# Scores of a gated linear recurrence in tiles of 32 keys on TensorE

## The chip, the cores and the metric

The kernel runs on one core of a Trainium2 chip. The metric is the device time of one execution in microseconds, the median of several runs. A core has a matmul engine (TensorE, PE in the profile, with its weight loads as PEld), VectorE (DVE), ScalarE (ACT), GpSimd (POOL), SyncE (SP, which issues most transfers here) and 16 DMA engines. Matmuls read from SBUF and write to PSUM, both with 128 partitions.

## What is computed

One block of a hybrid network on 1040 tokens (16 meta tokens and 1024 tokens) of width 1024: a layer norm, one large input projection, two recurrences side by side (HGRN2 with 8 heads of 128 keys and 128 values, mLSTM with 4 heads), their gated output projections, a layer norm, a mixture of 64 experts with 8 per token, and a last layer norm. The change touches only the first recurrence. For one head and one chunk of tokens it is, with `b` the running sum of the logarithms of the forget gate:

```python
b = jnp.cumsum(lfc, axis=2)
o_inter = jnp.einsum('bhtk,bhkv->bhtv', qc * jnp.exp(b), state)
rel = b[:, :, :, None, :] - b[:, :, None, :, :]
decay = jnp.exp(jnp.where(causal[:, :, None], rel, -jnp.inf))
scores = jnp.einsum('bhtk,bhsk,bhtsk->bhts', qc, kc, decay)
o = o_inter + jnp.einsum('bhts,bhsv->bhtv', scores, vc)
```

The decay depends on key, query and channel at once, so the scores are no plain matrix product of `q` and `k`.

## The kernel before

The kernel works on chunks of 128 tokens, 8 to a head, all 8 in one instruction where it can. Tokens lie on the free axis, the 128 key channels on the partitions. It splits the causal pairs of a chunk into levels. At level `lv` (block size B = 2^lv) the chunk is cut into blocks of B tokens; a query in an odd block meets the keys of the even block just ahead of it. Query and key are scaled by products of gates up to the border of the two blocks (`pre` and `suf`, which grow from level to level), so that the scores of a level are a plain matrix product. Level 0 (a query and the key one before it) and the diagonal (a query and its own key) are done together ahead of the loop.

*Diagonal and level 0* (line 699 to 706). `qx` holds for each chunk 128 queries and behind them the 64 odd queries times their gate, 192 columns. Line 704 multiplies all 128 keys of a chunk with all 192 columns, two chunks to a PSUM tile of the pool "sc" (`ps_sc()`, two buffers in turn), four groups a head. Lines 705 and 706 copy out of PSUM under a mask (`copy_predicated`) into `st`, the matrix of scores of the head: the diagonal from the first 128 columns, level 0 from the other 64.

*Levels 1 to 6* (line 707 on). Line 724 forms the scaled queries `qp` of the odd blocks, 64 a chunk, and line 726 the scaled keys of the even blocks in a tile `ks` whose other columns are zero or stale. Line 738 multiplies them: at levels 1 to 4 all 128 keys with all 64 queries of a chunk, 8 matmuls a level; at level 5 two matmuls a chunk, with 32 keys and 32 queries each, onto partitions 0 to 31 and 64 to 95 of PSUM; at level 6 one matmul a chunk with 64 keys and 64 queries, onto partitions 0 to 63. Levels 1 to 4 go through a masked copy of the whole tile on VectorE (line 741), since most of the 128 x 64 products of a chunk belong to no pair of that level: with blocks of up to 16 tokens, keys 32w to 32w+31 only meet the odd-block queries 16w to 16w+15. Levels 5 and 6 are copied by ScalarE (746, 747 and 749). Lines 752 to 756 carry `pre` and `suf` on to the next level, on VectorE. All these operands are float32.

Behind the levels, lines 767 to 798 turn the keys, carry the state from chunk to chunk and form the output of the head (line 790 reads `st`).

The order of the work is set by a planner when the kernel is built: it simulates the engines and takes, on each engine, the ready instruction of the highest priority. Each engine then runs its instructions in that order. PE's projections (lines 135 to 145, `mm3` and `mm_packed`, in `natural_slab`, `f_slab`, `q_slab`) are ready most of the time, and stand between the bursts of score matmuls. Heads 0 to 3 run beside the projections of the second half of the columns, heads 4 to 7 beside those of the second recurrence.

Of the kernel before, what the change touches and what calls it, by code (L numbers as in the profile page):

```python
# [14 lines left out]
AF = mybir.ActivationFunctionType  # L15
# [4 lines left out]
P = 128  # L20
# [51 lines left out]
def block_kernel(tc, A, out):  # L72
    nc = tc.nc
# [176 lines left out]
    def stage_tile():  # L250
        return stage.tile([P, 512], F32, name="st", tag="st", bufs=6)
# [325 lines left out]
    def ps_sc():  # L577
        return psum.tile([P, 512], F32, name="sc", tag="sc", bufs=2)
# [94 lines left out]
        nc.vector.tensor_mul(og, hn[:, :, 0:256], og)  # L673
        nc.sync.dma_start(tok(yB[:, hs]), og)

    def hgrn_head(h, kss, st, zero):
        hp = slice(h * P, (h + 1) * P)
        f = rt([P, L], "a0")
        qx = rt([P, 8, 192], "a1")
        q = qx[:, :, 0:P]  # L680
        nc.sync.dma_start(f, fT[hp, :])
        nc.sync.dma_start(q, qT[hp, :].rearrange("p (c t) -> p c t", t=P))
        v = rt([P, 8, P], "v")
        vm = rt([NM, P], "vm")
        g = rt([P, 8, P], "g")
        nc.sync.dma_start(v, tok(vA[NM:L, hp]))
        nc.sync.dma_start(vm, vA[0:NM, hp])
        nc.sync.dma_start(g, tok(gA[:, hp]))
        k = rt([P, L], "a2")
        nc.vector.tensor_scalar(k, f, -1.0, 1.0, op0=OP.mult, op1=OP.add)  # L690
        km = rt([P, NM], "km")
        nc.vector.memset(km[:, NM - 1:NM], 1.0)
        nc.vector.tensor_tensor_scan(km[:, NM - 2::-1], f[:, NM - 1:0:-1], zero[:, :NM - 1], 1.0, op0=OP.mult, op1=OP.add)
        nc.vector.tensor_mul(km, km, k[:, 0:NM])
        pre = f[:, NM:L].rearrange("p (c t) -> p c t", t=P)
        kx = k[:, NM:L].rearrange("p (c t) -> p c t", t=P)
        suf = rt([P, 8, P], "a3")

        nc.vector.tensor_mul(qx[:, :, P:], q[:, :, 1::2], pre[:, :, 1::2])
        for gg in range(4):  # L700
            sc = ps_sc()[:, 0:384].rearrange("p (c t) -> p c t", t=192)
            cs = slice(2 * gg, 2 * gg + 2)
            for i in range(2):
                nc.tensor.matmul(sc[:, i], kx[:, 2 * gg + i], qx[:, 2 * gg + i], start=True, stop=True)
            nc.vector.copy_predicated(st[:, cs], lmask[:, 5, 0:256].rearrange("p (c t) -> p c t", t=P), sc[:, :, 0:P])
            nc.vector.copy_predicated(st[:, cs, 1::2], lmask[:, 0, 0:128].rearrange("p (c t) -> p c t", t=64), sc[:, :, P:])
        for lv in range(7):
            B = 1 << lv
            N = 512 // B

            def sp(t):
                r = t.rearrange("p c (n w b) -> p (c n) w b", w=2, b=B)
                return r[:, :, 0, :], r[:, :, 1, :]

            p0, p1 = sp(pre)
            s0, s1 = sp(suf)
            if lv == 0:
                nc.gpsimd.tensor_copy(s0, p1)
                nc.gpsimd.memset(s1, 1.0)
                nc.vector.tensor_mul(p1, p1, p0[:, :, B - 1:B].to_broadcast([P, N, B]))  # L720
                continue
            qp = rt([P, N, B], "qp", 2)
            odd = [r.rearrange("p c (n w b) -> p c n w b", w=2, b=B)[:, :, :, 1] for r in (q, pre)]
            (nc.gpsimd if lv in QP_POOL else nc.vector).tensor_mul(qp.rearrange("p (c n) b -> p c n b", c=8), *odd)
            ks = kss[lv % 2]
            nc.vector.tensor_mul(sp(ks)[0], sp(kx)[0], s0)
            sc = ps_sc()
            qpf = qp.rearrange("p n b -> p (n b)")
            for c in range(8):
                t64 = c * 64  # L730
                if lv == 6:
                    spans = ((0, 64, 0, 64),)
                elif lv == 5:
                    spans = ((0, 32, 0, 32), (64, 96, 32, 64))
                else:
                    spans = ((0, P, 0, 64),)
                for a, b, u, v_ in spans:
                    nc.tensor.matmul(sc[a:b, t64 + u:t64 + v_], ks[:, c, a:b], qpf[:, t64 + u:t64 + v_],
                                     start=True, stop=True)
            if lv < 5:  # L740
                nc.vector.copy_predicated(sp(st)[1], lmask[:, lv].rearrange("p (n b) -> p n b", b=B),
                                          sc.rearrange("p (n b) -> p n b", b=B))
            else:
                scc = sc.rearrange("p (c t) -> p c t", t=64)
                if lv == 5:
                    nc.scalar.activation(st[0:32, :, 32:64], scc[0:32, :, 0:32], AF.Copy)
                    nc.scalar.activation(st[64:96, :, 96:128], scc[64:96, :, 32:64], AF.Copy)
                else:
                    nc.scalar.activation(st[0:64, :, 64:128], scc[0:64], AF.Copy)
            if lv == 6:  # L750

                nc.vector.tensor_mul(s1, s1, sp(kx)[1])
                nc.vector.tensor_mul(s0, sp(ks)[0], p1[:, :, B - 1:B].to_broadcast([P, N, B]))
            else:
                nc.vector.tensor_mul(s0, s0, p1[:, :, B - 1:B].to_broadcast([P, N, B]))
            nc.vector.tensor_mul(p1, p1, p0[:, :, B - 1:B].to_broadcast([P, N, B]))
        nc.vector.tensor_mul(q, q, pre)
        pt = ps_tr()
        nc.tensor.transpose(pt[:NM, 0], km, ident)
        knm = rt([NM, P], "knm")  # L760
        nc.scalar.activation(knm, pt[:NM, 0], AF.Copy)
        kn = rt([P, 8, P], "a5")
        for gg in range(2):
            n = 4 if gg == 0 else 3
            pt = ps_tr()
            for i in range(n):
                nc.tensor.transpose(pt[:, i], suf[:, 4 * gg + i], ident)
            nc.scalar.activation(kn[:, 4 * gg:4 * gg + n], pt[:, :n], AF.Copy)
        sts = rt([P, 8, P], "a2")
        pt = ps_tr()  # L770
        nc.tensor.matmul(pt[:, 0], knm, vm, start=True, stop=True)
        nc.vector.tensor_copy(sts[:, 0], pt[:, 0])
        for gg in range(2):
            n = 4 if gg == 0 else 3
            pt = ps_tr()
            for i in range(n):
                c = 4 * gg + i
                nc.tensor.matmul(pt[:, i], kn[:, c], v[:, c], start=True, stop=True)
            for i in range(n):
                c = 4 * gg + i  # L780
                nc.vector.scalar_tensor_tensor(sts[:, c + 1], sts[:, c], pre[:, c, P - 1:P], pt[:, i],
                                               op0=OP.mult, op1=OP.add)
        sq = rt([P, P], "sq", 2)
        ss = rt([P, 3, 8], "ss", 2)
        for gg in range(2):
            po = ps_tr() if gg else ps_o().rearrange("p (c t) -> p c t", t=P)
            s4 = slice(4 * gg, 4 * gg + 4)
            for i in range(4):
                c = 4 * gg + i
                nc.tensor.matmul(po[:, i], st[:, c], v[:, c], start=True, stop=False)  # L790
                nc.tensor.matmul(po[:, i], q[:, c], sts[:, c], start=False, stop=True)
            for i in range(4):
                nc.scalar.activation(sq, po[:, i], AF.Square, accum_out=ss[:, 0, 4 * gg + i:4 * gg + i + 1])
            nc.vector.tensor_scalar(ss[:, 1, s4], ss[:, 0, s4], 1.0 / P, EPS, op0=OP.mult, op1=OP.add)
            rsqrt(ss[:, 2, s4], ss[:, 1, s4], (P, 4))
            for i in range(4):
                c = 4 * gg + i
                nc.vector.scalar_tensor_tensor(g[:, c], po[:, i], ss[:, 2, c:c + 1], g[:, c], op0=OP.mult, op1=OP.mult)
        nc.sync.dma_start(tok(yA[:, hp]), g)
# [4 lines left out]
    with tc.tile_pool(name="reca", bufs=1) as rec:  # L804
# [2 lines left out]
        sts_ = [rec.tile([P, 8, P], F32, name=f"st{i}") for i in range(1)]  # L807
        for t in kss + sts_ + [zero]:
            nc.gpsimd.memset(t, 0.0)
        lm = stage_tile()[:, 0:384].rearrange("p (v t) -> p v t", t=64)  # L810
        nc.sync.dma_start(lm, A["lmask"])
        for lv in range(5):
# [4 lines left out]
        for s in range(2):  # L817
            if s:
                natural_slab(IA + s * 512, copy_out(vA, s * 512), True)
            natural_slab(GA + s * 512, gate_out(gA, s * 512, A["hg_norm_g"], True), False, None if s else slab_ga)  # L820
            f_slab(s)
            q_slab(s)
            for h in range(4):
                hgrn_head(4 * s + h, kss, sts_[0], zero)
        for s in range(2):
            natural_slab(VB + s * 512, copy_out(vB, s * 512), True)
            natural_slab(OB + s * 512, gate_out(oB, s * 512, A["ml_norm_g"], False), False)
# [713 lines left out]
    with man:  # L1541
# [10 lines left out]
        for t in range(N + 1):  # L1552
# [8 lines left out]
            if cur:  # L1561
                r = order[t][0]
# [296 lines left out]
```

## Time and profile before

| | |
|---|---|
| runs (3) | median 2410.21 us, 2406.28 to 2413.15 us |
| profiled execution | 2406.26 us, of which span 2404.5 us |
| PE busy | 2318.2 us, 96% of the span, 12754 matmul records |
| weight loads (PEld) | 1860.0 us, 77% |
| VectorE | 1587.8 us, 66% |
| ScalarE | 1106.7 us, 46% |
| GpSimd | 392.6 us, 16% |
| mean granted clock of PE | 0.984 |

The span is the time from the first to the last instruction. Busy time of PE counts a matmul from its start to its modelled end, and neighbours overlap, so a busy engine can still be made faster by shorter matmuls. A row of a timeline gives start, duration, engine, line, operation, tiles and shapes, and how many instructions were merged; a group's duration runs to the end of its last instruction. `128*32 128x32` is a matmul with 128 contraction rows, 32 weight columns and 32 moving columns.

### The profile page before, as it was taken

What the parts mean: (1) busy time and instruction counts of PE and PEld (TensorE: products, weight loads), DVE (VectorE), ACT (ScalarE), POOL (GpSimd) and SP (SyncE); (2) the same over time, 40 slices, a digit from 0 to 9 for tenths busy, and PEclk for the clock granted to TensorE, in tenths of its full rate; (3) what the DMA queues carried; (4) which work ended last, traced back from release to release, by engine and by line L of the source; (5) the groups of instructions that cost most, each with busy time, mean ns of one, the idle gap of its engine ahead of it and who ended that gap; (6) DMA issues with size and microseconds to landing.
All of it is one profiled execution on the core that took longest, in us unless ns stands there. A gap on an engine that the chain in (4) does not pass through costs nothing. (4 is left out here: it accounts for less than half of the span.)

```text
span 2404.5 us, 35446 instructions
## 1 busy us (share of the span) xinstructions
PE 2318.2 (96%) x12754; PEld 1860.0 (77%) x12754; DVE 1587.8 (66%) x3143; ACT 1106.7 (46%) x1848; POOL 392.6 (16%) x270
## 2 busy tenths in 40 slices
PE   6999999999999999999999999999999999999992
PEld 4788888988878987788788877777777777777761
DVE  8621888158812656412577596888888888888884
ACT  3432222221222246421332323777777777776773
POOL 3200000000000000000000001233434434444421
PEclk9989999999999999999999999999999999999996
DMA  7232333322323246526354425999999999999995
GB/s 277 89 106 88 106 111 115 119 93 89 102 96 107 79 160 206 175 97 216 129 201 144 135 85 188 299 334 317 337 324 327 312 333 321 314 324 322 306 291 157
DMA packets 203490, 476.71 MB, mean 198 GB/s; under 512 B 18721, under 2 KB 67553, under 8 KB 203313
## 3 DMA queue, kind: packets, MB, share of 16 engines
q1 hardware_dynamic: 181040, 396.24, 47.0%
q0 software_dynamic: 21520, 75.51, 13.4%
q10 hardware_dynamic: 752, 2.69, 0.3%
q8 instruction: 101, 1.65, 0.3%
q14 instruction: 77, 0.62, 0.1%
HBM read 372.16 MB, written 103.78 MB: 198 GB/s over the span
## 5 line engine op out<-in xcount | busy, mean ns | idle before, releaser
L197 DVE TENSOR_TENSOR wl<-wraw,wh 128x1024 fp32r<-128x1024 f32 x118 | 141.5, 1220 | 219.4 <-ACT wh L196 215.3
L136 PE MATMUL mm<-hL,wh 128*128 128x512 f32 (+2 forms) x768 | 278.0, 362 | 0.0
L137 PE MATMUL mm<-hH,wl 128*128 128x512 f32 (+2 forms) x768 | 277.5, 361 | 0.0
L135 PE MATMUL mm<-hH,wh 128*128 128x512 f32 (+2 forms) x768 | 277.0, 361 | 0.0
L1441 POOL DMA_INDIRECT acc<-yo,idx x95 | 193.3, 2035 | 504.3 <-DMA acc<-yo,idx 108.4
L137 PE MATMUL mm<-wh,hL 128*128 128x512 f32 x512 | 209.7, 410 | 6.3 <-DVE hL L346 6.3
L136 PE MATMUL mm<-wl,hH 128*128 128x512 f32 x512 | 209.4, 409 | 2.5 <-DVE wl L284 2.5
L135 PE MATMUL mm<-wh,hH 128*128 128x512 f32 x512 | 211.0, 412 | 0.6 <-DVE xr L534 0.6
L135 PEld LDWEIGHTS mm<-hH,wh 128*128 128x128 f32 x768 | 144.4, 188 | 17.1 <-issue 0.9
L136 PEld LDWEIGHTS mm<-hL,wh 128*128 128x128 f32 x768 | 144.4, 188 | 16.3 <-issue 0.5
L137 PEld LDWEIGHTS mm<-hH,wl 128*128 128x128 f32 x768 | 144.6, 188 | 15.6 <-issue 0.2
L196 ACT ACTIVATE wh<-wraw 128x1024 fp32r<-128x1024 f32 x118 | 122.7, 1056 | 57.9 <-PE mm L136 37.7
L1508 DVE TENSOR_TENSOR wl<-eraw,wh 128x1024 fp32r<-128x1024 f32 x112 | 134.9, 1215 | 17.0 <-ACT wh L1507 16.6
L1362 POOL DMA_INDIRECT xg<-h,idx x95 | 136.1, 1432 | 48.7 <-issue 23.5
L1508 DVE TENSOR_TENSOR wl<-wraw,wh 128x1024 fp32r<-128x1024 f32 x96 | 115.7, 1215 | 27.1 <-ACT wh L1507 26.7
L135 PE MATMUL mm<-wh,xh 128*128 128x512 f32 (+3 forms) x296 | 123.4, 417 | 0.0
L1507 ACT ACTIVATE wh<-eraw 128x1024 fp32r<-128x1024 f32 x112 | 117.0, 1060 | 13.6 <-PE mm L137 9.1
L137 PEld LDWEIGHTS mm<-wh,hL 128*128 128x128 f32 x512 | 98.6, 192 | 30.4 <-DVE hL L346 9.0
L137 PE MATMUL mm<-wh,xl 128*128 128x512 f32 (+3 forms) x296 | 116.6, 394 | 0.0
L136 PE MATMUL mm<-wl,xh 128*128 128x512 f32 (+3 forms) x296 | 116.5, 394 | 0.0
L136 PEld LDWEIGHTS mm<-wl,hH 128*128 128x128 f32 x512 | 98.8, 193 | 22.8 <-DVE wl L284 3.0
L135 PEld LDWEIGHTS mm<-wh,hH 128*128 128x128 f32 x512 | 99.0, 193 | 22.0 <-PE mm L530 0.8
(547 smaller groups left out, 5540.6 us busy)
## 6 DMA issues: line engine op xcount, KB each, us to landing
eraw<-in_wexp_dram SPq DMA_DIRECT2D x210, 512.0 KB, 7.7
wraw<-in_wexp_dram SPq DMA_DIRECT2D x168, 512.0 KB, 7.5
wraw<-in_w_in_dram SPq DMA_DIRECT2D x72, 512.0 KB, 5.0
sgT<-st SPq DMA_DIRECT2D x32, 256.0 KB, 2.5
sg<-sgT SPq DMA_DIRECT2D x32, 256.0 KB, 3.2
wraw<-in_w_branch_a_dram SPq DMA_DIRECT2D x16, 512.0 KB, 4.7
wraw<-in_w_branch_b_dram SPq DMA_DIRECT2D x16, 512.0 KB, 5.2
wraw<-in_w_out_dram SPq DMA_DIRECT2D x16, 512.0 KB, 4.0
```

The lines of the kernel that those rows point to most:

```text
L135: nc.tensor.matmul(o, ah, bh, start=start, stop=False)
L136: nc.tensor.matmul(o, ah, bl, start=False, stop=False)
L137: nc.tensor.matmul(o, al, bh, start=False, stop=stop)
L196: nc.scalar.activation(h, raw, AF.Copy)
L197: (nc.gpsimd if j in on_pool else nc.vector).tensor_sub(l, raw, h.bitcast(F32))
L1362: nc.gpsimd.indirect_dma_start(out=self.x, out_offset=None, in_=h1[:, :], in_offset=bass.IndirectOffsetOnAxis(ap=self.idx, axis=0))
L1441: self.out = nc.gpsimd.indirect_dma_start(out=acc[:, :], out_offset=bass.IndirectOffsetOnAxis(ap=self.idx, axis=0), in_=self.y, in_offset= ...
L1507: nc.scalar.activation(h, raw, AF.Copy)
L1508: (nc.gpsimd if j in POOL_SPLITS else nc.vector).tensor_sub(l, raw, h.bitcast(F32))
```

## The change

The scores of the diagonal and of levels 1 to 4 are computed in pieces of 32 keys, with only the queries that belong to those keys: four matmuls a chunk with 32 weight columns and 16 query columns at a level, eight a chunk (four with 32 query columns for the diagonal, four with 16 for level 0) ahead of the loop. Piece `w` writes partitions 32w to 32w+31 of PSUM. Level 6 keeps its matmul and puts odd chunks on partitions 64 to 127, so that ScalarE copies even and odd chunks apart. The products that no longer are computed leave parts of the PSUM tile unwritten; the tiles are therefore two fixed ones (`scs`), set to zero once, and no longer taken in turn from the pool: a group or level takes the one of its parity.

```diff
-    def hgrn_head(h, kss, st, zero):
+    def hgrn_head(h, kss, st, zero, scs):
...
         for gg in range(4):
-            sc = ps_sc()[:, 0:384].rearrange("p (c t) -> p c t", t=192)
+            sc = scs[gg % 2][:, 0:384].rearrange("p (c t) -> p c t", t=192)
             cs = slice(2 * gg, 2 * gg + 2)
             for i in range(2):
-                nc.tensor.matmul(sc[:, i], kx[:, 2 * gg + i], qx[:, 2 * gg + i], start=True, stop=True)
+                c = 2 * gg + i
+                for a, b in ((0, 32), (P, 16)):
+                    for w in range(4):
+                        r, u = slice(32 * w, 32 * w + 32), slice(a + b * w, a + b * w + b)
+                        nc.tensor.matmul(sc[r, i, u], kx[:, c, r], qx[:, c, u], start=True, stop=True)
...
-            sc = ps_sc()
+            sc = scs[lv % 2]
...
                 else:
-                    spans = ((0, P, 0, 64),)
+                    spans = tuple((32 * w, 32 * w + 32, 16 * w, 16 * w + 16) for w in range(4))
                 for a, b, u, v_ in spans:
-                    nc.tensor.matmul(sc[a:b, t64 + u:t64 + v_], ks[:, c, a:b], qpf[:, t64 + u:t64 + v_],
+
+                    o = 64 if lv == 6 and c % 2 else 0
+                    nc.tensor.matmul(sc[a + o:b + o, t64 + u:t64 + v_], ks[:, c, a:b], qpf[:, t64 + u:t64 + v_],
                                      start=True, stop=True)
...
-                    nc.scalar.activation(st[0:64, :, 64:128], scc[0:64], AF.Copy)
+                    for j in range(2):
+                        nc.scalar.activation(st[0:64, j::2, 64:128], scc[64 * j:64 * j + 64, j::2], AF.Copy)
...
+        scs = [ps_sc() for _ in range(2)]
+        for t in scs:
+            nc.vector.memset(t, 0.0)
...
-                hgrn_head(4 * s + h, kss, sts_[0], zero)
+                hgrn_head(4 * s + h, kss, sts_[0], zero, scs)
```

## Rows read from the trace of the kernel before

**Rows 1.** The page: busy time of PE; the granted clock in 40 slices.
```profile
PE 2318.2 (96%) x12754; PEld 1860.0 (77%) x12754; DVE 1587.8 (66%) x3143; ACT 1106.7 (46%) x1848; POOL 392.6 (16%) x270
...
PEclk9989999999999999999999999999999999999996
```

**Rows 2.** Table by stretches: length, busy us by engine (instructions), clock, DMA share, GB/s.
```profile
244.00:397.00 153.00, 151.84 (x1043) 127.93 (x1041) 128.46 (x305) 33.27 (x93) 4.21 (x7) 1.00 0.33 102
...
504.00:655.00 151.00, 149.65 (x1032) 125.86 (x1031) 125.98 (x301) 33.24 (x93) 3.63 (x6) 1.00 0.34 106
655.00:1400.00 745.00, 741.52 (x3553) 612.64 (x3553) 369.32 (x780) 248.15 (x429) 1.08 (x3) 1.00 0.42 143
```

**Rows 3.** Waits of VectorE, 244 to 655 us: total us, times, longest.
```profile
DVE st L741 <- PE sc L738: 25.3, 28, 1.4
```

**Rows 4.** Groups by form, PE, 244 to 655 us: busy us, mean ns, idle.
```profile
L738 PE MATMUL sc<-qp,kss 128*128 128x64 f32 x512 | 60.9, 273 | 0.6 <-DVE qp L724 0.2
...
L738 PE MATMUL sc<-qp,kss 128*64 128x64 f32 x128 | 9.2, 225 | 0.0
L738 PE MATMUL sc<-qp,kss 128*32 128x32 f32 x256 | 5.6, 197 | 0.0
```

**Rows 5.** PE's timeline around a burst of levels 1 to 4: start, duration, instruction.
```profile
294.28 0.40 PE L135 MATMUL mm<-wh,hH 128*128 128x512 f32 x1
294.51 0.39 PE L136 MATMUL mm<-wl,hH 128*128 128x512 f32 x1
...
296.76 0.39 PE L135 MATMUL mm<-wh,hH 128*128 128x512 f32 x1
```

**Rows 6.** PE's timeline around both diagonal bursts of head 1 (line 704).
```profile
280.30 0.40 PE L137 MATMUL mm<-wh,hL 128*128 128x512 f32 x1
...
282.07 0.39 PE L136 MATMUL mm<-wl,hH 128*128 128x512 f32 x1
...
282.76 0.39 PE L136 MATMUL mm<-wl,hH 128*128 128x512 f32 x1
...
284.79 0.40 PE L135 MATMUL mm<-wh,hH 128*128 128x512 f32 x1
```

**Rows 7.** PE's timeline around a burst of level 6.
```profile
350.08 0.39 PE L137 MATMUL mm<-wh,hL 128*128 128x512 f32 x1
350.41 1.15 PE L738 MATMUL sc<-qp,kss 128*64 128x64 f32 x16
...
351.82 0.38 PE L767 MATMUL tr<-ident,a 128*128 128x128 f32 x2
```

**Rows 8.** PE's timeline around a burst of level 5.
```profile
346.94 0.40 PE L136 MATMUL mm<-wl,hH 128*128 128x512 f32 x1
347.26 0.70 PE L738 MATMUL sc<-qp,kss 128*32 128x32 f32 x32
...
348.23 0.39 PE L135 MATMUL mm<-wh,hH 128*128 128x512 f32 x1
```

**Rows 9.** Stretches of 10 ns, line 738: PE, PEld; x counts instructions under way.
```profile
347.26:347.27 0.01, 0.01 (x1) 0.01 (x2) 1.00 0.53 205
...
350.46:350.47 0.01, 0.01 (x1) 0.01 (x2) 1.00 0.00 0
```

**Rows 10.** Line 749 (copies of level 6): ns minimum, median, maximum.
```profile
L749 ACT ACTIVATE st<-sc x8: 591/592/595, 267.3 to 652.8; 64x512 f32<-64x512 f32 x8
```

**Rows 11.** VectorE's timeline: masked copies of two successive levels, in brackets the idle time.
```profile
292.57 0.70 DVE L741 COPY_PREDICATED st<-lmask,sc 128x512 f32<-128x512 uint8 x1 [0.83 <-PE sc L738]
...
296.68 0.71 DVE L741 COPY_PREDICATED st<-lmask,sc 128x512 f32<-128x512 uint8 x1 [0.76 <-PE sc L738]
```

**Rows 12.** Timelines of VectorE and PE, head 2: last diagonal copies, burst of level 1.
```profile
325.13 0.72 DVE L706 COPY_PREDICATED st<-lmask,sc 128x128 f32<-128x128 uint8 x2
...
326.29 0.33 PE L738 MATMUL sc<-qp,kss 128*128 128x64 f32 x2
```

**Rows 13.** PE's timeline: a burst of matmuls of one column (line 929).
```profile
1444.26 0.34 PE L929 MATMUL po<-ones,selb 128*128 128x1 bf16 x8
```

## The prediction

> **What bounds the kernel now.** [...] The changed function runs in two stretches, heads 0 to 3 at 244 to 397 us and heads 4 to 7 at 504 to 655 us. PE is busy 151.8 of 153 us and 149.7 of 151 us in them, and 741.5 of 745 us in the stretch behind them [rows 2]. VectorE (DVE) comes second, 128 of 153 us and 126 of 151 us. The list of who waited for whom confirms it: in and between both stretches DVE waited 25.3 us for the score matmuls of levels 1 to 4 (28 times) [rows 3]. So PE is the bound, in and behind the changed part, and a microsecond of PE time taken out there should come off the end. How much PE time the scores hold is the whole question.
>
> Busy time does not answer it, since matmuls overlap (a record of a 64-column pass lasts 273 ns, 512 of them would be 140 us and are 60.9 us busy [rows 4]). I take the price of a burst of score matmuls from PE's timeline: from the start of the last projection matmul ahead of it to the start of the second one behind it, less 0.46 us for those two, which lie 0.23 us apart in a plain stream [rows 5]. It contains what the burst does to its neighbours.
>
> Every float32 matmul shows as two weight loads and two passes: the 256 matmuls of levels 1 to 4 give 512 records [rows 4].
>
> **Prices before.** A level of 1 to 4: 294.51 to 296.76 is 2.25, less 0.46: 1.79 us for 16 passes of 128 weight columns [rows 5]. There are 32 of these (8 heads, 4 levels). The diagonal: 280.30 to 282.07 gives 1.31 us, 282.76 to 284.79 gives 1.57 us, mean 1.44 us for 8 passes of 192 query columns [rows 6]; two such bursts a head, 16 in all. Level 6: 350.08 to 351.82 gives 1.28 us for 16 passes of 64 weight columns [rows 7]; 8 in all. Level 5 is not changed, and is the row to learn from: it already writes tiles of 32 keys, on partitions 0 and 64 in turn. 346.94 to 348.23 gives 0.83 us for 32 passes [rows 8], of which (0.70 - 0.197) = 0.50 us is the passes themselves (from the first one's start to the last one's; one lasts 197 ns [rows 4]) and 0.33 us the change from and to the full-width matmuls. That is 15.8 ns a pass, where a level of 1 to 4 takes 1.79/16 = 112 ns.
>
> **Do tiles of 32 keys run side by side?** The onset of the two bursts tells it. At level 5 two weight loads are under way in the first 10 ns; at level 6, all on one tile, the second one joins 50 to 60 ns behind the burst's start at 350.41 [rows 7, 9]. By the order of the code the first two loads of level 5 would be the two passes of the same 32 keys. Had they shared one tile, the second would have come as late as at level 6 does, scaled to 32 columns. So I read the pair as the first passes of the tiles at partitions 0 and 64: each tile goes through its own passes at 0.50/16 = 31.5 ns, and the two tiles go at once.
>
> **The change, part by part.** *Levels 1 to 4.* 8 matmuls become 32, four tiles by 8 chunks: 64 passes, 16 to a tile, exactly what each tile of level 5 gets, with 16 query columns instead of 32. If four tiles go at once as two do, a level costs what level 5 costs: 0.83 us. Saved: 0.96 x 32 = 30.7 us. *Diagonal.* Two groups are 4 chunks of 8 matmuls, 64 passes, again 16 to a tile: 0.83 us; saved (1.44 - 0.83) x 16 = 9.8 us. *Level 6.* As many matmuls, now on partitions 0 and 64 in turn: half of 15 steps (1.15 - 0.225 = 0.93 us [rows 4, 7]) is 0.46 us; x 8 = 3.7 us. Sum 44.2 us of PE time.
>
> *Edits at next to nothing.* ScalarE copies level 6 in two pieces instead of one of 592 ns [rows 10]; that adds less than another 592 ns a head, on an engine that is busy 33 of 153 us [rows 2]. Two memsets of a score tile on DVE come once, ahead of the first head, and only its first scores wait for them; by the copies of 512 columns (0.70 us [rows 11]) they are 1.4 us if uncovered. The masked copies from PSUM keep their shapes. PE's stream grows by 152 matmuls a head, 2432 passes and as many loads in all. No DMA is added or moved.
>
> *One buffer order changes.* The diagonal's last group and level 1 now share a score tile, so level 1 waits for that group's four masked copies. In head 2 these end at 325.13 + 0.72 = 325.85 and level 1's burst begins at 326.29 [rows 12]: covered by 0.44 us now, and the diagonal ends sooner after the change. Queued behind that wait would be projection matmuls. I take 0; uncovered, four copies (1.5 us) x 8 heads is 12 us.
>
> **Bounds of the unknown price.** No row has four tiles at once. Above: passes issue no closer than level 5's average of 15.8 ns. Below: half the query columns shorten the passes, and a tile's 31.5 ns could shrink up to half, 0.25 us a level or 8 to 10 us in all. I take the tile's own pace, since the onset [rows 9] shows passes 10 ns apart or less and nothing there that two tiles share.
>
> **Rivals.**
> *Issue pace.* If 15.8 ns is what PE can issue, 64 passes take 1.01 + 0.33 = 1.34 us. Saved: 0.45 x 32 + 0.10 x 16 + 3.7 = 19.7 us. For it: level 5's 64 instructions may have been queued while PE was busy, and 128 in a row are nowhere in the trace.
> *A new wait.* From one level's masked copy to the next DVE works 3.4 of 4.11 us (292.57 to 296.68; five operations of 0.68 to 0.70 us, the first and the next copy stand in the rows) and waits 0.76 us for PE [rows 11]. PE spends 1.79 us of the 4.11 on the burst; with 0.83 us and the same projection matmuls it would be round in 3.15 us, and wait 0.3 us for DVE: 9.6 us of 32 levels, leaving 34.6 us. Against it: the planner sets the order anew and has projection matmuls to put in.
> *The floor (slower).* A pass never starts less than 25 ns behind the last one. For it: eight 1-column matmuls of the router take (0.34 - 0.163)/7 = 25 ns each [rows 13]. Then 64 passes take 1.60 + 0.33 = 1.93 us: 0.14 x 32 + 0.49 x 16 - 3.7 = 8.6 us lost. It decides from 22 ns on, where 48 x (64 passes + 0.33 us) equals the 84 us of today, level 6's gain included. Against it: level 5's 15.8 ns. The router's matmuls all use one tile. [...]
> *The tiles do not run side by side* (the change does not do what it says): 64 x 31.5 ns + 0.33 = 2.35 us, 0.56 x 32 + 0.91 x 16 = 32.5 us lost, level 6 gaining nothing. Level 5 speaks against it.
> *Nothing arrives.* The new order of the planner delays a projection or its weights by as much as is saved. Against it: no idle stretch of PE lies behind the part [rows 2].
>
> **How the numbers follow.** The profiled execution took 2406.26 us, the median of the runs is 2410.21, 3.95 us more. Forecast: 2406.26 - 44.2 = 2362.1, on the median 2366 us; chance 0.45. New wait: 2376, 0.18. Issue pace: 2390, 0.18. Nothing arrives: 2410, 0.08. The floor: 2419, 0.07. No side by side: 2443, 0.04. The range goes from 2356 (the shorter pass) to 2398 (issue pace with some waiting), and leaves out the last three, 0.19. About 0.3%, 7 us, is what a measurement of this kernel can tell from no change: faster 0.81, same 0.08, slower 0.11.
>
> **What would show it.** The burst of levels 1 to 4 should last some 0.7 us with 64 passes, the diagonal's as long, level 6 about 0.7 us; PE should count 2432 more matmuls and wait as little as now; the second stretch should end about 44 us earlier, and what follows keep its length. Bursts of 1.2 us mean the issue pace, of 1.8 us the floor. PE waiting for DVE at the score lines means the new wait. The prediction is wrong if the bursts shrink and the end does not move.

## The result, and the profile after

The changed kernel took 2380.8 us (median of 4 runs, 2374.28 to 2384.78), the kernel before beside it 2411.68 us: ratio 0.9873, 95% interval 0.985 to 0.9896, or 30.6 us less (this and all such figures below go by the ratio). The direction was right and the time lies in the range; of the 44 us forecast, 14 are missing. The profiled execution took 2378.61 us, its span 2376.8 us, 27.7 us less than before.

The page of the changed kernel, PE's line and the granted clock in 40 slices:

```profile
PE 2277.3 (96%) x15186; PEld 1808.1 (76%) x15186; DVE 1587.0 (67%) x3145; ACT 1106.6 (47%) x1856; POOL 385.9 (16%) x270
...
PEclk9989999999999999999999999999999999999996
...
q8 instruction: 120, 1.97, 0.3%
```

PE counts 2432 more matmul records than in [rows 1], as expected, and is 40.9 us less busy. That is more than the 27.7 us by which the span fell, so PE must now wait somewhere. The table by stretches (columns as in [rows 2]) shows where:

```profile
244.00:397.00 153.00, 145.91 (x2261) 114.11 (x2258) 131.08 (x312) 36.99 (x101) 4.17 (x7) 0.98 0.35 108
504.00:655.00 151.00, 146.46 (x2046) 115.75 (x2045) 129.01 (x330) 40.31 (x116) 3.61 (x6) 1.00 0.37 114
655.00:1400.00 745.00, 738.75 (x3542) 609.41 (x3541) 380.25 (x847) 246.04 (x420) 1.08 (x3) 1.00 0.42 141
```

In [rows 2] PE was idle 1.2 and 1.4 us in these two stretches; now it is idle 7.1 and 4.5 us. The third row no longer holds the same work as before; counted from the start of the last score matmul to the end, PE is idle 62.3 us where it was 60.6, so most of the new idle time lies in the two stretches. The list of PE's waits in the same stretches (line waited for: us in total, times, longest), all of it:

```profile
PE sc L708 <- DMA a<-qT: 6.1, 5, 1.5
PE sc L744 <- issue: 4.6, 3, 3.8
PE sc L708 <- DVE kss L730: 0.7, 1, 0.7
PE sc L744 <- DVE qp L728: 0.5, 3, 0.2
```

Two of them are new and large: the diagonal (line 708) waits for the load of the queries, and the levels (line 744) wait for "issue", which is nothing that the profile names.

PE's timeline around one burst of levels 1 to 4, and around one of level 6 (start, duration, instruction; compare [rows 5, 7]):

```profile
295.44 0.40 PE L135 MATMUL mm<-wh,hH 128*128 128x512 f32 x1
295.77 0.74 PE L744 MATMUL sc<-qp,kss 128*32 128x16 f32 x64
...
296.78 0.40 PE L137 MATMUL mm<-wh,hL 128*128 128x512 f32 x1
...
304.96 0.40 PE L135 MATMUL mm<-wh,hH 128*128 128x512 f32 x1
305.29 0.69 PE L744 MATMUL sc<-qp,kss 128*64 128x64 f32 x16
...
306.24 0.39 PE L137 MATMUL mm<-wh,hL 128*128 128x512 f32 x1
```

Priced as in the prediction, a level costs 296.78 - 295.44 - 0.46 = 0.88 us (median of 28 bursts 0.87), where 0.83 was forecast and 1.79 was paid. Its 64 passes begin within 0.55 us, on average one every 0.55/64 = 8.6 ns. Level 6 costs 306.24 - 304.96 - 0.46 = 0.82 us (forecast 0.81, before 1.28). Both shapes do what they were meant to do.

Now the two waits. First the diagonal of head 1: SyncE's issue of the queries' load, then PE.

```profile
276.81 0.57 SPq L682 DMA_DIRECT2D a<-qT  x1
...
280.56 0.39 PE L137 MATMUL mm<-wh,hL 128*128 128x512 f32 x1
281.69 0.33 PE L708 MATMUL sc<-a,a 128*32 128x32 f32 x16 [0.74 <-DVE kss L730]
...
282.29 0.39 PE L136 MATMUL mm<-wl,hH 128*128 128x512 f32 x1
...
283.19 0.61 PE L708 MATMUL sc<-a,a 128*32 128x16 f32 x48
```

Sixteen passes that take 0.14 us cost 282.29 - 280.56 - 0.46 = 1.27 us, because the queries land 4.7 us behind their issue (at 281.56 us) and PE stands in front of them. (The bracket names a VectorE instruction; the other five of these waits are put down to the load itself. In all six heads this first burst starts 0.14 us behind the landing in the trace.) The diagonal of a head is now three bursts, of 16, 48 and 64 passes, instead of two.

Second, head 0, in PE's timeline:

```profile
247.81 1.18 PE L744 MATMUL sc<-qp,kss 128*32 128x16 f32 x79
252.78 0.93 PE L744 MATMUL sc<-qp,kss 128*32 128x16 f32 x49 [3.79 <-issue]
...
254.23 0.63 PE L137 MATMUL mm<-wh,hL 128*128 128x512 f32 x1
254.66 0.63 PE L135 MATMUL mm<-wh,hH 128*128 128x512 f32 x1
```

The stretches ahead of the stop and behind it, in the table by stretches, PE alone (length, busy us, instructions, granted clock, DMA share, GB/s):

```profile
244.00:248.90 4.90, 4.68 (x158) 1.00 0.94 289
252.70:258.10 5.40, 5.32 (x60) 0.50 0.02 5
```

Levels 1 and 2 stand back to back here, 128 passes, and PE stops 3.79 us in their middle. Behind the stop the granted clock is 0.50 for 5.4 us: projection matmuls lie 0.43 us apart instead of 0.23.

The prices of all bursts, summed for each kernel by the prediction's method (us; stops and waits inside a burst are part of its price):

| kernel | diagonal | levels 1 to 4 | level 6 | sum | span | span less sum |
|---|---|---|---|---|---|---|
| before | 22.8 | 59.3 | 10.2 | 92.3 | 2404.5 | 2312.2 |
| after | 23.4 | 34.7 | 6.6 | 64.7 | 2376.8 | 2312.1 |
| levels only (e1) | 25.6 | 28.0 | 6.5 | 60.1 | 2373.4 | 2313.3 |
| diagonal only (e2) | 24.3 | 59.3 | 10.2 | 93.8 | 2406.5 | 2312.7 |
| queries in two buffers (e3) | 16.5 | 32.8 | 6.5 | 55.8 | 2370.4 | 2314.6 |
| level 1 of two heads whole (e4) | 26.7 | 32.8 | 6.6 | 66.1 | 2378.2 | 2312.1 |
| tile after tile (e5) | 27.0 | 68.5 | 6.6 | 102.1 | 2416.0 | 2313.9 |
| tiles of 64 (e6) | 25.2 | 41.1 | 6.6 | 72.9 | 2385.6 | 2312.7 |
| e1 and two buffers (e7) | 23.0 | 28.8 | 6.5 | 58.3 | 2371.7 | 2313.4 |
| e3 and e4 (e8) | 17.1 | 32.7 | 6.5 | 56.3 | 2371.1 | 2314.8 |
| e3, two diagonals whole (e9) | 17.5 | 28.2 | 6.6 | 52.3 | 2362.2 | 2309.9 |
| e3, instructions shifted (e10) | 16.4 | 33.6 | 6.5 | 56.5 | 2374.9 | 2318.4 |
| before, two buffers (e11) | 23.9 | 57.5 | 10.2 | 91.6 | 2399.1 | 2307.5 |

The last column is nearly constant (2312 to 2315 in ten of the thirteen, 2307.5 to 2318.4 in all): to within some 5 us, a microsecond of burst price is a microsecond of span. The clock outside the changed part also differs between single executions: ahead of the first head the mean granted clock was 0.76 before and 0.80 after from 120 to 155 us, and from 0 to 244 us 0.94 before, 0.95 after, 0.98 in e7 and 0.97 in e9. That it explains the rest is not shown: e7, with the highest, has 2313.4 in the last column. So the forecast's frame holds, and the question is the terms: the diagonal saved -0.6 us instead of 9.8, the levels 24.6 instead of 30.7, level 6 3.6 of 3.7.

### The profile page after: what moved, and what is told of

Its sections match the earlier page's. It is cut to its first block, busy times and chain, and to the rows that moved or that the text cites. A ratio compares the mean times of both kernels' runs of the same rounds, so it can differ in the third digit from the quotient of the medians.

```text
span 2376.8 us, 40262 instructions
## 1 busy us (share of the span) xinstructions
PE 2277.3 (96%) x15186; PEld 1808.1 (76%) x15186; DVE 1587.0 (67%) x3145; ACT 1106.6 (47%) x1856; POOL 385.9 (16%) x270
## 5 line engine op out<-in xcount | busy, mean ns | idle before, releaser
L135 PEld LDWEIGHTS mm<-wh,hH 128*128 128x128 f32 x512 | 98.8, 193 | 22.8 <-PE mm L530 1.1
```

The source lines that it names most:

```text
L135: nc.tensor.matmul(o, ah, bh, start=start, stop=False)
```

## Experiments

**Which part gained.** The change was split in two.

e1, the diagonal undone:

```diff
-                for a, b in ((0, 32), (P, 16)):
-                    for w in range(4):
-                        r, u = slice(32 * w, 32 * w + 32), slice(a + b * w, a + b * w + b)
-                        nc.tensor.matmul(sc[r, i, u], kx[:, c, r], qx[:, c, u], start=True, stop=True)
+                nc.tensor.matmul(sc[:, i], kx[:, c], qx[:, c], start=True, stop=True)
```

> Levels 1 to 4 in tiles of 32 keys and level 6 on two tiles in turn, as in the change; the diagonal as before, one matmul of 192 query columns a chunk. Theory A (the diagonal's share of the gain was eaten by a new wait for the next head's queries): the diagonal costs what it cost before, 22.8 us of PE time, as its pieces cost now with their waits (23.4 us), so this kernel keeps the whole gain, 27 to 31 us under the kernel before. Rival B (the diagonal does give its 10 us, and as much was lost somewhere in the levels): 17 to 20 us under the kernel before.

Measured: 2375.51 us, ratio 0.986 (0.9843 to 0.9877), 33.7 us less than before. Leaving the diagonal's tiles out costs nothing (the intervals of this kernel and of the whole change overlap). Its whole diagonals cost 25.6 us, 2.8 more than before: PE waits 2.4 us, in five places, for the product of line 699, which follows the queries; before, it was 0.4 us once. The stop in head 0 is gone too; its two levels back to back, in PE's timeline:

```profile
246.92 1.59 PE L741 MATMUL sc<-qp,kss 128*32 128x16 f32 x128
```

e2, the levels undone (diagonal alone):

```diff
-                    spans = tuple((32 * w, 32 * w + 32, 16 * w, 16 * w + 16) for w in range(4))
+                    spans = ((0, P, 0, 64),)
...
-                    o = 64 if lv == 6 and c % 2 else 0
+                    o = 0
...
```

> Only the diagonal in tiles of 32 keys; levels 1 to 4 and 6 as before. Theory A (new wait for the queries): no gain, within 3 us of the kernel before, and PE waits 1 to 2 us ahead of the first diagonal burst of six heads. Rival B: 8 to 10 us under the kernel before.

Measured: 2404.76 us, ratio 0.9977 (0.9966 to 0.9989), 5.5 us less. In its trace the diagonal gains nothing (24.3 us) and its span is 2 us longer than before; the profiled execution, 2408.31 us, lies near the upper end of its runs. PE's wait list has the same new row:

```profile
PE sc L708 <- DMA a<-qT: 7.7, 5, 2.0
```

So the gain of the diagonal's tiles is eaten in the diagonal itself, by waiting for queries. The 5.5 us of the runs lie between the two expectations, and the trace doesn't show where they come from.

**The wait for the queries.** `qx` has one buffer, so a head's queries can be called for only when the last output matmul of the head ahead has read them (276.39 us for head 0, issue at 276.81). e3 gives `qx` a second buffer and finds room for it in another tile:

```diff
-        qx = rt([P, 8, 192], "a1")
+        qx = rt([P, 8, 192], "a1", 2)
...
+        qps = rt([P, 2, 512], "a5")
...
-            qp = rt([P, N, B], "qp", 2)
+            qp = qps[:, lv % 2].rearrange("p (n b) -> p n b", b=B)
```

> The changed kernel with two buffers for the query tile, so that the next head's queries can be loaded before the last matmul of this head has read its own (room is made by putting the two query products of the levels into the tile that later takes the turned keys). Theory A: the wait ahead of the first diagonal burst (some 7 to 9 us over six heads) goes, so 6 to 10 us under the changed kernel, 36 to 41 us under the kernel before. Rival (PE waits there for VectorE, which is late with the keys, and not for the load): no change against the changed kernel.

Measured: 2365.66 us, ratio 0.9823 (0.9809 to 0.9837), 42.7 us less than before (36 to 41 expected). The row of the queries has left PE's wait list; this is all of it:

```profile
PE sc L745 <- issue: 3.8, 2, 3.4
PE sc L709 <- DVE a L690: 1.3, 3, 0.8
PE sc L745 <- DVE a L729: 0.2, 1, 0.2
```

The diagonal's price falls from 23.4 to 16.5 us. Two controls ask whether the second buffer, and not the diagonal, brought this. e7 is e1 with two buffers:

> The diagonal undone (whole matmuls of 128 keys and 192 queries) and the queries in two buffers: the same as the run with the queries in two buffers but for the diagonal. Theory A (the diagonal's tiles are worth what was forecast once the queries lie ready, less the stop for instructions in head 0): slower than that run by 5 to 10 us, about 2371 to 2376 us, -34 to -39 us to the kernel before, hardly other than without the second buffer (2375.5 us), since whole diagonal matmuls waited little for the queries. Rival B (the second buffer of the queries by itself brings the gain, and the diagonal's tiles bring none): equal to that run, about 2366 us.

Measured: 2372.83 us, ratio 0.9841 (0.9824 to 0.9858). By the trace the diagonal's tiles are now worth 23.0 - 16.5 = 6.5 us, of which the stop in head 0 takes back 4.0 (levels 28.8 against 32.8); the runs differ by 7 us with overlapping intervals. The whole diagonals, 25.6 us in e1, are back at 23.0. e11 is the kernel before with two buffers:

> The kernel before with the queries in two buffers and nothing else. Theory A (the wait for the queries came only with the change, since the whole diagonal needed the product of line 699 and was placed later): 0, within 3 us of the kernel before. Rival B (the second buffer is a gain of its own, and the run with the change and two buffers owes it that): -6 to -12 us.

Measured: 2404.31 us, ratio 0.9989 (0.9975 to 1.0003): no change that can be told, and a gain of more than 6 us is excluded. The second buffer is worth something only where the change has put the wait.

**Four tiles at once.** e5 computes the same 32 matmuls of a level in another order, all chunks of one tile, then the next tile:

```diff
-            for c in range(8):
...
-                for a, b, u, v_ in spans:
+            for c, (a, b, u, v_) in ([(c, s) for s in spans for c in range(8)] if lv < 5 else [(c, s) for c in range(8) for s in spans]):
```

> The kernel of the change with one edit: at levels 1 to 4 the loop over the four tiles stands outside and the loop over the eight chunks inside, so that the same 32 matmuls come tile after tile instead of the four tiles in turn. Theory A (the 8.6 ns a pass come from four tiles at work at once, and they are that only because consecutive matmuls go to different tiles): a tile's own pace is 31.5 ns a pass (level 5), 64 passes in a row on one tile after the other take 2.02 us plus 0.33 us, a level 2.35 us net instead of 0.87; x 28 to 32 levels that is 41 to 47 us over the change, some 2422 to 2428 us, slower than the kernel before. Rival B (PE takes matmuls for an idle tile ahead of those for a busy one, or a small pass costs no more on the same tile): 0.87 us a level as in the change, 2381 us, within 3 us.

Measured: 2414.36 us, ratio 1.0019 (1.0002 to 1.0037): the whole gain is gone. PE's timeline:

```profile
291.18 0.40 PE L135 MATMUL mm<-wh,hH 128*128 128x512 f32 x1
291.50 1.90 PE L742 MATMUL sc<-qp,kss 128*32 128x16 f32 x64
...
293.67 0.39 PE L137 MATMUL mm<-wh,hL 128*128 128x512 f32 x1
```

A level costs 293.67 - 291.18 - 0.46 = 2.03 us; its 64 passes take 1.72 us, 27 ns a pass instead of 8.6, so the same matmuls are 3.1 times as fast when the four tiles come in turn. Theory A holds, but 27 ns is not the pace of one tile. Within a tile the trace's records start 31.7 ns apart, as at level 5 (31.5), so passes of 16 query columns follow each other no faster than passes of 32. The mean is lower because of the three borders between tiles: there the first three passes of the next tile start between the last four of the tile ahead, each within 6 ns of one of those. The expectation of 2.35 us had no such overlap. So PE does let passes for an idle tile go ahead here, as Rival B has it, but only three at each border; the starts recorded there are not in the order of the program. The first 16 passes of e5, on one tile, begin within 0.50 us; 64 on four tiles in turn begin within 0.55 us.

e6 takes two tiles of 64 keys and 32 queries, half as many matmuls:

```diff
-                    spans = tuple((32 * w, 32 * w + 32, 16 * w, 16 * w + 16) for w in range(4))
+                    spans = tuple((64 * w, 64 * w + 64, 32 * w, 32 * w + 32) for w in range(2))
```

> The kernel of the change with one edit: levels 1 to 4 in two tiles of 64 keys with their 32 queries instead of four of 32 keys with 16; 16 matmuls and 32 passes a level instead of 32 and 64. Theory A (a burst lasts as long as the passes of one tile at that tile's own pace): level 6 on one tile took (1.15 - 0.225) us / 15 steps = 0.062 us a pass of 64 keys in the kernel before; 16 passes a tile, two tiles at once, are 0.99 us plus 0.33 us, a level 1.3 us instead of 0.87: +12 to +14 us of 28 to 32 levels, less the stop of 3.8 us in head 0 and half of the smaller ones if fewer instructions don't run into it: 2387 to 2395 us. Theory B (the count of passes decides, 8.6 ns each): 32 passes take 0.28 us plus 0.33 us, a level 0.61 us: -8 us of the levels, -5 us of the stop: about 2368 us.

Measured: 2385.49 us, ratio 0.9893 (0.9871 to 0.9914).

```profile
284.53 0.39 PE L136 MATMUL mm<-wl,hH 128*128 128x512 f32 x1
284.85 1.12 PE L744 MATMUL sc<-qp,kss 128*64 128x32 f32 x32
...
286.25 0.39 PE L135 MATMUL mm<-wh,hH 128*128 128x512 f32 x1
```

286.25 - 284.53 - 0.46 = 1.26 us a level, with half the passes of the change: the pace of a tile (58 ns a pass of 64 keys) sets the price, not the count of passes. Level 6 of the kernel before has the same 58 ns with 64 query columns in place of 32. So in these shapes a tile's pace goes by its keys (weight columns) and not by its queries: 31.7 ns for 32 keys with 16 queries (31.5 with 32), 58 ns for 64 keys with 32 or 64. No stop occurs in this kernel, which has 1024 passes fewer, and that gives back part of the loss.

**The stop in head 0.** e4 makes level 1 of heads 0 and 4 whole again:

```diff
-                    spans = tuple((32 * w, 32 * w + 32, 16 * w, 16 * w + 16) for w in range(4))
+                    spans = ((0, P, 0, 64),) if lv == 1 and h % 4 == 0 else tuple((32 * w, 32 * w + 32, 16 * w, 16 * w + 16) for w in range(4))
```

> The changed kernel, but in heads 0 and 4 level 1 is computed with 128 keys at once (8 matmuls for 32). There levels 1 and 2 stand back to back, and in head 0 PE stopped for 3.9 us in the middle of the 128 passes. Theory F (PE ran out of fetched instructions): with 80 passes in place of 128 the stop goes or shrinks under 1 us, and with it the matmuls at half the clock behind it: 4 to 6 us under the changed kernel, after paying 0.9 us in each of the two heads. Rival (the stop comes from a wait on another engine): the stop stays, 0 to 2 us over the changed kernel.

Measured: 2375.55 us, ratio 0.986 (0.9845 to 0.9876). The stop shrinks to 1.02 us, but a whole level 1 costs more than one of tiles (1.79 us in the kernel before, 0.87 in the changed one), and in its trace PE waits 8.3 us for the queries instead of 6.1; the interval overlaps that of the change. e8 is e3 and e4 together:

> Both remedies at once: queries in two buffers, and level 1 of the first head of each half in whole matmuls of 128 keys (heads 0 and 4 only). Theory A (the two losses are separate: the wait for the queries and PE's stop for its instructions in head 0 with the lower clock behind it): 2 to 5 us faster than with the two buffers alone, 2361 to 2364 us, -46 to -49 us to the kernel before, and the granted clock of the stretch 252 to 258 us stays near 1. Rival B (the stop only moves to the next dense stretch of instructions, or the two whole levels cost what the stop took): within 2 us of the run with two buffers, about 2366 us.

Measured: 2373.24 us, ratio 0.9833 (0.9815 to 0.985), not faster than e3: the back-to-back levels of heads 0 and 4 cost 8.0 us, with the stops 8.1. Rival B is right that nothing is gained over e3; its 2366 us is 7 us under the median here, and the intervals of e3 and e8 overlap.

But these runs gave a clue. Counted over all of PE's records from the start (weight loads, passes and the few semaphore waits between them), PE stopped behind the same record, the 2497th, in the changed kernel, in e3, e4, e5 and e8, although other work lay there. Here are e3 and e4 in PE's timeline:

```profile
247.75 1.18 PE L745 MATMUL sc<-a,kss 128*32 128x16 f32 x79
252.34 0.93 PE L745 MATMUL sc<-a,kss 128*32 128x16 f32 x49 [3.42 <-issue]
```

```profile
243.37 2.94 PE L744 MATMUL sc<-qp,kss 128*32 128x16 f32 x79
247.33 0.20 PE L744 MATMUL sc<-qp,kss 128*32 128x16 f32 x1 [1.02 <-issue]
```

In these traces PE's instructions come by DMA: the page counts 120 transfers on queue 8 after the change and 101 before, 19 more, of 16 KB each; and 2 x 2432 = 4864 more records (a load and a pass for each) are 19 x 256. In e1, e2 and e6 3072, 1792 and 2816 more records than before come with 12, 7 and 11 more transfers, again 256 to one. So in these kernels a transfer is a block of 256 instructions. The times at which the block's transfer is first seen in the trace's DMA records, against the time at which PE went on (us):

```
kernel   block seen at   PE goes on at   later by
after        250.28          252.78         2.5
e3           250.05          252.34         2.3
e4           245.07          247.33         2.3
e8           250.04          252.47         2.4
e10          490.87          493.11         2.2
```

And what the DMA engines did meanwhile in the changed kernel, two stretches of the DMA view (queue: packets, MB, share of 16 engines), 243.5 to 250.2 us and 250.2 to 252.7 us:

```profile
q1 hardware_dynamic: 1082, 2.07, 94.3%
...
q1 hardware_dynamic: 47, 0.07, 8.9%
q8 instruction: 1, 0.02, 2.4%
```

The block came when the weights' transfers ended. It is so in other traces too: queue 1 fills 99.8% of the engines' time from 241 to 245 us in e4 (block seen at 245.07) and 99.8% from 487.9 to 490.8 us in e10 (490.87). Two experiments test that the stop is an end of a block, and no property of 128 small passes. e9 is e3 with the diagonal of heads 0 and 4 whole, 224 instructions fewer ahead of these levels:

```diff
+                if h % 4 == 0:
+                    nc.tensor.matmul(sc[:, i], kx[:, c], qx[:, c], start=True, stop=True)
+                    continue
```

> Queries in two buffers, and the diagonal of the first head of each half (heads 0 and 4) in whole matmuls of 128 keys, all else as in the change: 224 instructions of PE fewer ahead of the levels of each of these two heads. Theory A (in head 0 PE runs out of instructions, since a block of 256 of them is fetched behind the weights that are under way until 250 us; with fewer instructions ahead, PE reaches the end of its block only after the fetch): no stop at level 1 or 2 of head 0, the two levels back to back 1.7 us as in the runs with whole diagonals instead of 5.9, head 4's the same; two diagonals dearer by 0.6 us each; together 3 to 4 us less than with two buffers alone, 2362 to 2364 us, -46 us to the kernel before, and the granted clock stays near 1 behind it. Rival B (128 small passes in a row stop PE by themselves): the stop of 3.4 to 3.8 us stays, 2367 us.

Measured: 2366.26 us, ratio 0.9815 (0.9798 to 0.9832), 44.6 us less than before. No stop at these levels, and the clock stays up: here too the block is seen only when the weights' transfers thin out, at 245.40 us, but PE comes to its 2497th record as late as 248.4 us. PE's timeline:

```profile
243.38 1.58 PE L748 MATMUL sc<-a,kss 128*32 128x16 f32 x128
```

The stretches around it, PE alone (columns as above):

```profile
237.00:250.00 13.00, 12.88 (x243) 1.00 0.59 185
250.00:262.00 12.00, 12.00 (x163) 1.00 0.13 46
```

The span is the shortest of all (2362.2 us); from 0 to 244 us, ahead of the first head, the granted clock was 0.97 in this execution and 0.95 in the changed kernel's and e3's. Between the medians of e9 and e3 nothing can be told.

e10 is e3 with 32 matmuls of zeros ahead of the first head, which push all later instructions back by 128 places:

```diff
+        for i in range(32):
+            nc.tensor.matmul(scs[0][0:16, 0:16], zero, zero, start=True, stop=True)
```

> Queries in two buffers, and 32 matmuls of zeros (16 x 16; 64 weight loads and 64 passes) put in long before the first head, so that every later instruction of PE stands 128 places further back in the stream; nothing near head 0 is changed. In the four runs with a stop PE stopped behind the same record of its trace, the 2497th, whether that lay in level 1 or in level 2. Theory A (the stop is the end of a block of 256 instructions): again near the 2497th record, now 128 records earlier in the program, at the first records of level 1; that block is called for some 2 us earlier, ahead of the weights' transfers at 243 us, so the fetch lands before PE comes there, and the stop is under 1 us or gone. The block behind it ends 26 records into the projection matmuls after the two levels. Rival B (the burst of 128 passes itself, or a wait that belongs to its place in the program): the stop stays behind the same matmul of the program and lasts 3 to 4 us. The matmuls of zeros cost at most 2 us; the time is no test, the trace is: about 2364 to 2368 us.

Measured: 2373.76 us, ratio 0.9844 (0.9826 to 0.9862), above the 2364 to 2368 us expected. PE's timeline in head 0 and in head 4:

```profile
249.09 1.51 PE L745 MATMUL sc<-a,kss 128*32 128x16 f32 x128
...
488.52 1.42 PE L745 MATMUL sc<-a,kss 128*32 128x16 f32 x119
493.11 0.30 PE L745 MATMUL sc<-a,kss 128*32 128x16 f32 x9 [3.17 <-issue]
```

The stretch behind the second, PE alone:

```profile
493.30:496.50 3.20, 3.20 (x16) 0.50 0.02 5
```

The same 128 passes of head 0 run through without a stop once the block ends elsewhere. The stop has not vanished but moved: head 4, whose stops were 0.25 and 0.61 us in the changed kernel, now stops 3.17 us, with the lower clock behind it, and a burst near 576 us stops 1.8 us. Counted as above, these two stops lie behind records 8385 and 10945, and the two of head 4 in the changed kernel behind 8129 and 8385: 22, 23 and 33 whole blocks of 256 behind the 2497th. That is Theory A with a place that it did not name.

What stays open: that the fetch waits *because* the weights' transfers fill the DMA engines is read from their ending together in these traces; it was not tried alone. It is no strict rule either: in head 0 of e10 the block is seen at 246.55 us, with queue 1 at 91% from 244.8 to 246.5 us and at 96% in the 2 us behind.

## Why the prediction came out as it did

*The bound.* Right. Span less burst price lies within 3 us in ten of the thirteen kernels, so PE's time in the bursts was the whole question.

*Tiles of 32 keys side by side.* Right, 0.87 us a level where 0.83 was forecast. The onset of level 5 [rows 9] was read correctly, and the chosen value, a tile's own pace, was the better end: 64 passes took 0.55 us against 0.50. The lower bound, that half the query columns shorten the passes, is answered by e5: 31.7 ns a pass on one tile, where level 5 has 31.5 with 32 columns. Issue pace (1.34 us), floor (1.93 us) and tiles in sequence (2.35 us) are refuted for tiles in turn. The floor's 25 ns [rows 13] is not contradicted on one tile, where e5's passes lie 31.7 ns apart, but it does not hold across tiles: in the burst at 295.77 us of the changed kernel the records start 6 to 7 ns apart within each of the first eight rounds of four, and 0 to 17 ns apart behind them.

*Levels 1 to 4, 30.7 us.* Mis-sized by the stops alone: 24.6 us with them; 31.3 in e1 and 31.1 in e9, whose levels have none.

*Level 6, 3.7 us.* Right, 3.6.

*The diagonal, 9.8 us: the step that failed.* "64 passes, again 16 to a tile: 0.83 us" priced the matmuls and left the place of the burst as it was. The whole matmul needed both halves of `qx`, so also the product of line 699 (0.69 us), and in the trace of before the queries had landed 0.8 to 1.1 us ahead of the first burst in heads 1 to 3 and 5 to 7. Cut in pieces, the first 32-query matmuls need only queries and keys; the planner put them as early as that allowed, in front of a load that is issued when the head ahead is done. (The shorter levels add to it: by themselves they make whole diagonals 2.8 us dearer in e1.) "No DMA is added or moved" was true, but a matmul was moved ahead of one. With the wait taken away (e3) the term is 6.4 us. Of the rest, 24 bursts instead of 16, at 0.33 us for each change of shape as at level 5 [rows 8], make some 2.6 us, an estimate, and 1.3 us of short waits remain in e3.

*PE's stream.* The prediction counted "152 matmuls a head" more and gave them no price beside the passes. They cost a stop of 3.8 us and, as an estimate, some 1.8 us at the lower clock behind the burst (nine projection matmuls from 254.23 to 258.07 us, 0.20 us late each), besides two smaller stops in head 4.

*The rivals.* "A new wait" was the right kind at the wrong place: PE waits only 0.5 us for the scaled queries, and VectorE's wait for scores fell from 25.3 us [rows 3] to 10.8 us, 5.2 of them the stop:

```profile
DVE st L747 <- PE sc L744: 10.8, 11, 5.2
```

The score tile that the diagonal and level 1 share cost nothing, as taken.

*The sum.* 44.2 us was right for the mechanism, but that e9, with the two losses gone, is 44.6 us faster than before is in part luck: its bursts save 40.0 us, 5.3 us of diagonal instead of 9.8, and in its profiled execution some 2 us come from outside the bursts.

*The signs.* The second stretch was to end 44 us earlier and what follows to keep its length. The last score matmul starts 20.2 us earlier (652.6 and 632.4 us), and what follows is 7.5 us shorter, with 40 fewer of PE's matmul records behind it in the planner's new order. So this sign could not measure the gain.

## What to carry to other kernels

The small matmuls paid here when consecutive ones went to different column tiles (0.87 us a level, 1.79 with whole matmuls); the same matmuls tile after tile gave everything back (2.03 us), so look at the order before the shape. When a matmul is cut so that a piece depends on less, ask where the scheduler will put that piece and which load then ends last: a buffer that was early enough for the whole may be late for the piece (here PE came to wait 6.1 us for the queries). Many small instructions are also a transfer (here 4864 more records came with 19 more transfers of 16 KB, 256 to one): count them in such blocks and see what the DMA engines do when a dense stretch crosses the end of one.

## What the hardware showed that I had not expected

PE stopped in the middle of a burst with no wait for data in the profile: 3.8 us (after), 3.4 (e3), 3.2 and 1.8 (e10), 1.8 (e5), 1.5 (e8) and 1.0 (e4). The five stops of the table above ended 2.2 to 2.5 us after the next block of 256 instructions was first seen on queue 8. Behind the stops of the changed kernel and of e5 the granted clock was 0.50 for 5.4 and 6.6 us, behind that of e3 0.51 over 6.0 us, behind the longer one of e10 0.50 for 3.2 us; behind those of e8 and e4 it was 1.00.

Passes of 32 keys started 31.7 ns apart on one tile with 16 queries (e5), as with 32 (31.5 ns at level 5); on four tiles in turn 64 of them began within 0.55 us (after), hardly more than the 0.50 us of 16 on one tile. When the same 64 came tile after tile (e5) they took 1.72 us, since only three passes overlapped at each border.
